# Moving the first four gate tiles of an RG-LRU branch forward among a projection's matmuls, with new pools

## The chip, the cores and the metric

The kernel runs on one core of one Trainium2 chip. Its time is the device time in microseconds (us) from one execution; of several executions the median is given. The engines that matter are TensorE (PE, the matmuls), VectorE (DVE), ScalarE (ACT) and GpSimd (POOL); SyncE (SP) issues most of the DMAs, ACT a few.

## The reference: one layer of a hybrid recurrent decoder

576 tokens (one prompt of 512 and 8 samples of 8) of width 1024 go through one layer. One projection of the normed input yields the columns of three branches and of three merge gates; each branch ends in a SiLU gate and an output projection, and the merged sum goes through one more.

```python
u, za, xb, zb, q, zc, gates = split_in(xn @ w_in)
oa = rwkv7_branch(u, za, ...); ob = rglru_branch(xb, zb, ...); oc = cross_attn(q, zc, mem_k, mem_v)
merged = g_a * (oa @ w_br_a) + g_b * (ob @ w_br_b) + g_c * (oc @ w_br_c)
y = x + merged @ w_out
```

The branch that the change touches is the RG-LRU ("Hawk"): a causal convolution of width 4 over `xb`, two block-diagonal gates, a linear recurrence over time, and the product with SiLU(zb):

```python
xc = conv_b + sum(ext[:, j:j + t] * cw[j] for j in range(4))
a = exp(-8 * sigmoid(xc @ w_rg_a + b) * softplus(-lam))
b = sqrt(1 - a * a) * sigmoid(xc @ w_rg_x + b2) * xc
h_t = a_t * h_(t-1) + b_t;  out = h * silu(z)
```

## The kernel before: a stream of projections with everything else between

**The stream.** Every big projection is cut into units of 128 output columns. A unit (class `Unit`, run by `Stream.step`, L355) has 8 steps, one for each 128 rows of the contraction; a step is 6 matmuls of 288 tokens (three products of high and low parts, two halves of the tokens), so a unit is 48 matmuls. Its weights are loaded by SP (`wraw`), rounded by ACT (`whi`, L280), and the rest is made by DVE (`wlo`, L281); the stream does this for the next unit when a unit starts, if a next unit is queued. A unit writes one of two PSUM buffers and ends in a `use`: for `zb` a tanh on ACT and a multiply on DVE (L410, L411) and a store to DRAM; for a branch unit `br` one multiply on DVE (L448 or L450), and for the middle branch an addition on POOL (L452). `st.go(n)` emits n steps, `st.until(label)` emits until a unit is done.

**The order of work** at the end of the kernel: the RWKV phase, among whose operations the units of the gates, of `zc` and `xb` and the first two of `zb` run; the other six `zb` units; 8 units `br2` (branch c, "first", which write `merged`), 8 units `br0` (branch a, "mid"), 8 units `br1` (branch b, the LRU's, "last"), and the output projection (L1345). `br1` needs the LRU's output `ob` as high and low parts (`oh`, `ol`).

**The LRU phase** (`lru_phase`, L468 on) works on 8 tiles of 128 channels. For tile j, `conv(j)` loads `xe` (issued by ACT, L490), and makes `xc` with one ACT and four DVE instructions (L496 to L502) and two small POOL copies; `gates(j)` is 4 small products on PE (`pg`, L516; the trace shows 8 records), 4 tanh on ACT (L517), three DVE instructions (L521, L530, L532) and four more ACT ones (L525 to L529), and leaves the decay `ae`, the gated input `gx` and the argument of a root; `roots` takes the square roots of four tiles in one ACT instruction (L557); `scan(j)` makes `be` on POOL (L542 to L544), runs the recurrence on DVE (L546), copies two state columns on POOL (L548, L549), multiplies with the gate path `z` on DVE (L551, L552) and splits the product into `oh` and `ol` (L592 on ACT, L593 on DVE). `load_split` loads a branch's output from DRAM and splits it in the same way.

**What sets the order.** The program text gives each instruction its rank; a planner then simulates the engines with its own costs and writes each engine's queue: an instruction that it takes to be ready can pass one of a higher rank that is not. The queues are fixed in that order before the kernel runs, and each engine keeps its order. Tiles live in pools; a tile whose buffer or memory is still in use waits for the last reader of the one before.

In the kernel before, `lru_phase` is called when all `zb` units are written and the input `xh`, `xl` is released (`xstack.close()`). Its main loop is

```python
for j in range(4):
    conv(j); st.go(9 if j else 13); gates(j)
    if j == 3: then()
    st.go(3)
st.until("br27"); roots(0)
for j in range(4, KC):
    conv(j); st.go(4); scan(j - 4); st.go(3); gates(j); st.go(3)
roots(4)
for j in range(4, KC):
    scan(j); st.go(9)
```

Of the kernel before, what the change touches and what calls it, by code (L numbers as in the profile page):

```python
# [9 lines left out]
F32 = mybir.dt.float32  # L10
F32R = mybir.dt.float32r
I32 = mybir.dt.int32
AF = mybir.ActivationFunctionType
ALU = mybir.AluOpType
# [4 lines left out]
P = 128  # L19
D = 1024  # L20
KC = 8
TP = 512
NB = 8
NS = 8
N = TP + NB * NS
# [359 lines left out]
def smp(t):  # L385
    return t[:, TP:N].rearrange("p (b s) -> p b s", s=NS)
# [78 lines left out]
        split(nc, oh[:, k, :], ol[:, k, :], t)  # L465


def lru_phase(K, o2, then):  # L468
    nc, tc, i, pv = K.nc, K.tc, K.i, K.pv
    st = K.st  # L470
    lo_st = K.cst.tile([P, 9, 8], F32, name="lru_st")
    cv_st = K.cst.tile([P, 9, 3, 8], F32, name="conv_st")
    with tc.tile_pool(name="lruc", bufs=1, reuse_waits="tile") as lc, tc.tile_pool(name="lru", bufs=2, reuse_waits="tile") as lp:
        wbd = []
        for q, nm in enumerate(("w_rg_a", "w_rg_x")):
            w = lc.tile([P, KC, P], F32, name=f"wbd{q}")
            nc.gpsimd.memset(w, 0.0)
            src = i[nm][0].rearrange("(j two) i o -> two i j o", two=2)
            for h in range(2):
                nc.scalar.dma_start(w[64 * h:64 * h + 64, :, 64 * h:64 * h + 64], src[h])  # L480
            wbd.append(w)
        AE = TP + NB * 9
        ohl = []
        sl = K.par[:, K.off["state_lru"]:K.off["state_lru"] + 64].rearrange("p (b j) -> p b j", j=8)
        xcs, keep, args, quad = {}, {}, {}, {}

        def conv(j):
            xe = lp.tile([P, XE], F32, tag="xe", name="xe")
            xp, xs = token_ext(xe, 3)
            nc.scalar.dma_start(xe, K.xbd[j])  # L490
            nc.gpsimd.tensor_copy(cv_st[:, 0, :, j], xp[:, TP:TP + 3])
            nc.gpsimd.tensor_copy(cv_st[:, 1:9, :, j], xs[:, :, NS:NS + 3])
            t = lp.tile([P, XE], F32, tag="cva", name="cva")
            M = XE - 3
            cw = [pv("conv_w", r * 8 + j) for r in range(4)]
            nc.scalar.activation(t[:, :M], xe[:, 0:M], AF.Identity, scale=cw[0], bias=pv("conv_b", j))  # L496
            for r in (1, 2):
                nc.vector.scalar_tensor_tensor(t[:, :M], xe[:, r:r + M], cw[r], t[:, :M], op0=ALU.mult, op1=ALU.add)
            xc = lp.tile([P, N], F32, tag="xc", name="xc")
            nc.vector.scalar_tensor_tensor(xc[:, 0:TP], xe[:, 3:3 + TP], cw[3], t[:, 0:TP], op0=ALU.mult, op1=ALU.add)  # L500
            ts = t[:, 515:515 + 88].rearrange("p (b s) -> p b s", s=11)[:, :, 0:8]
            nc.vector.scalar_tensor_tensor(smp(xc), xs[:, :, 3:], cw[3], ts, op0=ALU.mult, op1=ALU.add)  # L502
            xcs[j] = xc

        def gates(j):
            if j % 4 == 0:
                quad[j // 4] = lp.tile([P, 4, N], F32, tag="args", name="args")
            ar = args[j] = quad[j // 4][:, j % 4, :]
            xc = xcs[j]
            gs = []  # L510
            for q, bh in enumerate((K.bah, K.bxh)):
                g = lp.tile([P, N], F32, tag=f"g{q}", name=f"g{q}")
                for s in range(2):
                    pg = K.psb(f"pg{q}")[:, 0:HN]
                    cs = slice(HN * s, HN * s + HN)
                    nc.tensor.matmul(pg, wbd[q][:, j, :], xc[:, cs], start=True, stop=True)  # L516
                    nc.scalar.activation(g[:, cs], pg, AF.Tanh, bias=bh[:, j:j + 1], scale=0.5)  # L517
                gs.append(g)
            gr, gi = gs
            c4 = K.c4[:, j:j + 1]  # L520
            nc.vector.tensor_scalar(gr, gr, c4, c4, op0=ALU.mult, op1=ALU.add)  # L521
            ae = lp.tile([P, AE], F32, tag="ae", name="ae", bufs=4)
            ap_, as_ = token_ext(ae, 0, 9)
            nc.gpsimd.memset(as_[:, :, 0:1], 0.0)
            nc.scalar.activation(ap_, gr[:, 0:TP], AF.Exp)  # L525
            nc.scalar.activation(as_[:, :, 1:9], smp(gr), AF.Exp)
            th = lp.tile([P, AE], F32, tag="th", name="th")[:, 0:N]
            nc.scalar.activation(th, gr, AF.Tanh, scale=-1.0)
            nc.scalar.activation(gr, gr, AF.Exp, scale=2.0)  # L529
            nc.vector.scalar_tensor_tensor(ar, gr, 1.0, th, op0=ALU.add, op1=ALU.mult)  # L530
            gx = lp.tile([P, N], F32, tag="gx", name="gx", bufs=4)
            nc.vector.scalar_tensor_tensor(gx, gi, 1.0, xc, op0=ALU.add, op1=ALU.mult)  # L532
            keep[j] = (ae, gx)

        def scan(j):
            ar = args[j]
            ae, gx = keep[j]
            z2 = o2.tile([P, N], F32, tag="gtt", name="z2", bufs=5)
            K.dma(z2, K.zbd[j])
            be = lp.tile([P, AE], F32, tag="th", name="be")  # L540
            bp_, bs_ = token_ext(be, 0, 9)
            nc.gpsimd.tensor_copy(bs_[:, :, 0:1], sl[:, :, j:j + 1])  # L542
            nc.gpsimd.tensor_mul(bp_, ar[:, 0:TP], gx[:, 0:TP])
            nc.gpsimd.tensor_mul(bs_[:, :, 1:9], smp(ar), smp(gx))  # L544
            he = lp.tile([P, XE], F32, tag="cva", name="he")[:, 0:AE]
            nc.vector.tensor_tensor_scan(he, ae, be, 0.0, op0=ALU.mult, op1=ALU.add)  # L546
            hp_, hs_ = token_ext(he, 0, 9)
            nc.gpsimd.tensor_copy(lo_st[:, 0, j:j + 1], hp_[:, TP - 1:TP])  # L548
            nc.gpsimd.tensor_copy(lo_st[:, 1:9, j:j + 1], hs_[:, :, 8:9])  # L549
            o = lp.tile([P, N], F32, tag="g0", name="lo")  # L550
            nc.vector.scalar_tensor_tensor(o[:, 0:TP], hp_, 0.5, z2[:, 0:TP], op0=ALU.mult, op1=ALU.mult)  # L551
            nc.vector.scalar_tensor_tensor(smp(o), hs_[:, :, 1:9], 0.5, smp(z2), op0=ALU.mult, op1=ALU.mult)  # L552
            split(nc, ohl[0][:, j, :], ohl[1][:, j, :], o)

        def roots(j0):
            q4 = quad[j0 // 4]
            nc.scalar.activation(q4, q4, AF.Sqrt, scale=0.25)  # L557

        for j in range(4):
            conv(j)  # L560
            st.go(9 if j else 13)
            gates(j)
            if j == 3:
                then()
            st.go(3)
        st.until("br27")
        ohl = [o2.tile([P, KC, N], F32R, tag=tag, name=tag) for tag in ("oh", "ol")]
        roots(0)
        for j in range(4, KC):
            conv(j)  # L570
            st.go(4)
            scan(j - 4)
            st.go(3)
            gates(j)
            st.go(3)
        roots(4)
        for j in range(4, KC):
            scan(j)
            st.go(9)
    lf = lo_st.rearrange("p a b -> p (a b)")  # L580
    K.rows_out(lf, [(0, 72, [(0, 8, K.o["lru_p"].rearrange("a b (j c) -> (a b j) c", c=P)),
                             (8, 64, K.o["lru_s"].rearrange("a b (j c) -> (a b j) c", c=P))])])
    cf = cv_st.rearrange("p a r b -> p (a r b)")
    cs = K.o["conv_s"].rearrange("a b r (j c) -> (a b r j) c", c=P)
    K.rows_out(cf, [(0, 120, [(0, 24, K.o["conv_p"].rearrange("a b r (j c) -> (a b r j) c", c=P)), (24, 96, cs[0:96])]),
                    (120, 96, [(0, 96, cs[96:192])])])
    return ohl
# [795 lines left out]
def hybrid_step(ctx: ExitStack, tc: tile.TileContext, ins, outs):  # L1383
    nc = tc.nc
    K = Kern(ctx, tc, ins, outs)
    st = K.st = Stream(K)

    def pool(stack, name, bufs=1, **kw):
        return stack.enter_context(tc.tile_pool(name=name, bufs=bufs, reuse_waits="tile", **kw))
# [52 lines left out]
    rwkv_phase(K)  # L1442
    for j in range(KC):
        st.until(f"zc{j}")
    K.merged = pool(ctx, "mg").tile([P, KC, N], F32, name="merged")
    o2 = pool(ctx, "o2", bufs=2)

    def operand():
        return [o2.tile([P, KC, N], F32R, tag=tag, name=tag) for tag in ("oh", "ol")]

    oc, oa = operand(), operand()
    load_split(K, o2, K.ocz, *oc)
    for j in range(KC):
        st.until(f"zb{j}")
    xstack.close()
    st.add(*branch_units(K, o2, 2, ins["w_br_c"][0], *oc, "first"))
    st.add(*branch_units(K, o2, 0, ins["w_br_a"][0], *oa, "mid"))
    ob = lru_phase(K, o2, lambda: load_split(K, o2, K.oad, *oa))
    st.until("br07")
    mhl = operand()  # L1460
    st.add(*branch_units(K, o2, 1, ins["w_br_b"][0], *ob, "last", mhl))
    with ExitStack() as es:
        fp = pool(es, "fin")
# [40 lines left out]
```

## Time and profile before

| | |
|---|---|
| time, median of 3 | 1185.82 us (1184.57 to 1187.84) |
| the profiled execution's own time | 1189.67 us |
| its span, first to last instruction | 1187.9 us |
| PE busy | 1151.5 us (97%) |
| DVE, ACT, POOL busy | 711.5, 516.0, 182.7 us |
| mean granted TensorE clock | 0.992 |

In the profile a row of the timeline gives start, duration, engine, line, operation, output and inputs, how many instructions are merged in the row, and in brackets the idle time before it with the instruction that ended it. Matmuls overlap, so the rhythm of PE is read from one start to the next. A group row gives busy time, the mean duration in ns, and the idle time before the group with what ended it. In a table by stretches the columns are the length and then, for PE, weight loads, DVE, ACT and POOL, the busy time with the number of instructions; then the granted clock, the DMA share and GB/s.

### The profile page before, as it was taken

The page shows a single profiled execution, that of the slowest core. Times are in us where ns is not written, and L with a number is a line of the kernel's source. Part 1 is how long each engine was busy: PE and PEld are TensorE (multiplying, and loading weights), DVE is VectorE, ACT ScalarE, POOL GpSimd, SP SyncE. Part 2 cuts the span into 40 slices and gives each one's busy share as a digit, 9 for nine tenths or more (in the row PEclk, how much of TensorE's full clock was granted, in tenths as well). Part 3 has the DMA queues.
Part 4 walks back from the last instruction along what each step waited for, and adds up shares of the span by engine and source line. Part 5 has one row for each costly group of instructions (what it writes and reads, how often), then busy time and mean ns, then how long its engine had stood idle before and what let it go on. Part 6 is the DMA issues. An engine that isn't in the chain of part 4 may idle for free.

```text
span 1187.9 us, 25753 instructions
## 1 busy us (share of the span) xinstructions
PE 1151.5 (97%) x10599; PEld 1070.9 (90%) x10599; DVE 711.5 (60%) x1435; ACT 516.0 (43%) x1003; POOL 182.7 (15%) x311
## 2 busy tenths in 40 slices
PE   6999999999999999999999999999999999989997
PEld 4998877898998898988989988999889999979997
DVE  5445655238754687735788457875355386875633
ACT  5444544337224473243742335622434366542333
POOL 3010001010003210022100130102211011570032
PEclk9999999999999999999999999999999999999999
DMA  4447685532342222432224522254336666338412
GB/s 139 129 142 226 219 252 189 158 89 79 87 134 78 68 88 77 139 87 65 72 84 134 136 81 66 82 145 128 98 99 206 202 209 180 104 105 268 112 50 81
DMA packets 219344, 150.99 MB, mean 127 GB/s; under 512 B 52384, under 2 KB 194826, under 8 KB 219226
## 3 DMA queue, kind: packets, MB, share of 16 engines
q1 hardware_dynamic: 215962, 146.34, 42.1%
q10 hardware_dynamic: 3264, 2.99, 0.9%
q8 instruction: 84, 1.38, 0.5%
q14 instruction: 34, 0.28, 0.1%
HBM read 120.29 MB, written 29.01 MB: 126 GB/s over the span
## 4 chain that ended last, share of the span: by engine, by line
PE 81%; DVE 7%; ACT 4%; issue 3%; DMA 3%; POOL 1%; SPq 0%; DVEq 0%; ACTq 0%
PE u L355 13%; PE g L355 12%; PE br L355 9%; PE za L355 5%; PE xb L355 4%; PE zc L355 4%; PE q L355 4%; PE fo L1345 4%; PE zb L355 3%; PE kv L355 2%; PE dS L1133 1%; PE m L986 1%; DVE wlo L281 1%; DMA wraw<-in_w_mem_kv 1%; PE skt L64 1%
## 5 line engine op out<-in xcount | busy, mean ns | idle before, releaser
L280 ACT CAST whi<-wraw 128x1024 fp32r<-128x1024 f32 x129 | 135.4, 1050 | 300.6 <-PE g L355 87.9
L281 DVE TENSOR_TENSOR wlo<-wraw,whi 128x1024 fp32r<-128x1024 f32 x128 | 158.4, 1237 | 130.7 <-ACT whi L280 123.6
L355 PE MATMUL u<-xh,whi 128*128 128x288 f32 x400 | 93.3, 307 | 0.0
L355 PE MATMUL u<-xh,wlo 128*128 128x288 f32 x400 | 89.6, 299 | 0.0
L355 PE MATMUL u<-xl,whi 128*128 128x288 f32 x400 | 88.5, 299 | 0.0
L355 PE MATMUL br<-oh,whi 128*128 128x288 f32 x384 | 85.0, 303 | 3.0 <-ACT oh L592 2.9
L355 PE MATMUL br<-oh,wlo 128*128 128x288 f32 x384 | 83.8, 300 | 4.0 <-DVE wlo L281 4.0
L355 PE MATMUL g<-xh,whi 128*128 128x288 f32 x384 | 85.8, 302 | 0.0
L355 PE MATMUL g<-xh,wlo 128*128 128x288 f32 x384 | 84.4, 298 | 0.0
L355 PE MATMUL g<-xl,whi 128*128 128x288 f32 x384 | 84.4, 299 | 0.0
L355 PE MATMUL br<-ol,whi 128*128 128x288 f32 x384 | 83.7, 300 | 0.0
L355 PEld LDWEIGHTS u<-xh,whi 128*128 128x128 f32 x400 | 65.0, 188 | 6.9 <-issue 5.3
L355 PEld LDWEIGHTS br<-oh,wlo 128*128 128x128 f32 x384 | 62.7, 192 | 5.4 <-DVE wlo L281 5.3
L355 PEld LDWEIGHTS br<-oh,whi 128*128 128x128 f32 x384 | 63.2, 192 | 4.3 <-ACT oh L592 3.4
L355 PEld LDWEIGHTS u<-xh,wlo 128*128 128x128 f32 x400 | 65.2, 188 | 0.8
L355 PEld LDWEIGHTS u<-xl,whi 128*128 128x128 f32 x400 | 64.9, 188 | 0.8 <-issue 0.4
L355 PEld LDWEIGHTS g<-xh,whi 128*128 128x128 f32 x384 | 61.7, 188 | 3.3 <-issue 3.1
L355 PEld LDWEIGHTS g<-xl,whi 128*128 128x128 f32 x384 | 62.1, 188 | 1.6 <-issue 1.6
L355 PEld LDWEIGHTS br<-ol,whi 128*128 128x128 f32 x384 | 63.1, 192 | 0.1
L355 PEld LDWEIGHTS g<-xh,wlo 128*128 128x128 f32 x384 | 62.2, 188 | 0.9 <-issue 0.9
L1012 DVE TENSOR_TENSOR Xt<-X 72x30 f32<-72x30 f32 (+14 forms) x120 | 39.4, 328 | 13.6 <-DMA X<-d 9.9
L1345 PE MATMUL fo<-wol,oh 128*128 128x256 f32 (+1 forms) x160 | 45.0, 282 | 0.0
(388 smaller groups left out, 2895.3 us busy)
## 6 DMA issues: line engine op xcount, KB each, us to landing
wraw<-in_w_in SPq DMA_DIRECT2D x89, 512.0 KB
wraw<-in_w_mem_kv SPq DMA_DIRECT2D x16, 512.0 KB
kn<-in_cache_mem_k SPq DMA_DIRECT2D x16, 512.0 KB
kn<-in_cache_mem_v SPq DMA_DIRECT2D x16, 512.0 KB
gd<-flt SPq DMA_DIRECT2D x24, 288.0 KB
gtt<-gd SPq DMA_DIRECT2D x24, 288.0 KB
wraw<-in_w_br_c SPq DMA_DIRECT2D x8, 512.0 KB
wraw<-in_w_br_a SPq DMA_DIRECT2D x8, 512.0 KB
```

The lines of the kernel that those rows point to most:

```text
L64: self.nc.tensor.transpose(out, in_, self.ident[:rows, :rows])
L280: nc.scalar.copy(hi, raw)
L281: eng.tensor_sub(lo, raw, hi.bitcast(F32))
L355: nc.tensor.matmul(self.ps[:, o:o + m], a[:, k, :], b[:, k, t0:t0 + m], start=(k == 0 and q == 0), stop=(k == KC - 1 and q == 2))
L986: nc.tensor.matmul(pms[h][64 * w:64 * w + 64, P * (c - c0):P * (c - c0) + P], BK[64 * h:64 * h + 64, c, w, :], ZR[64 * h:64 * h + 64, c].r ...
L1012: nc.vector.tensor_mul(tv, X[:, 0:s, s:s + 1].to_broadcast([NQ, s, m]), X[:, s:s + 1, s + 1:].to_broadcast([NQ, s, m]))
L1133: nc.tensor.matmul(pS[hs, C * o.q:C * o.q + C], o.BKn[:, c, hs], o.UV[:, c, hs], start=True, stop=True, tile_position=(0, 64 * h))
L1345: nc.tensor.matmul(pos[t][:r, :W], a[:, k, t * P:t * P + r], b[:, k, :], start=(k == 0 and q == 0), stop=(k == KC - 1 and q == 2))
```

## The change

`lru_phase` is now called before the six remaining `zb` units have been emitted. The convolutions and gates of tiles 0 to 3 are emitted among these units (6 steps, gates, 4 steps for each tile: 40 of 48 steps). Then `zb` is finished, `merge()` releases `xh` and `xl`, allots `merged` and the operand of branch a in the place of the input, and queues `br2` and `br0`. The scans of tiles 0 to 3 follow with 3 steps between, the convolutions and gates of tiles 4 to 7 with 5, `load_split` of branch a (`then()`), and the scans of tiles 4 to 7 with 4. A scan no longer splits its result: the product is written over `gx`, which has 8 buffers now, and after `br27` the 8 splits are emitted together, with 3 steps between, among the `br0` units. The root's argument has one buffer of four tiles where it had two; `oh`, `ol` of branch c are in a pool of one buffer, which the LRU's operand takes over, and those of branch a are in another, which the merged operand takes over.

```diff
-def lru_phase(K, o2, then):
+def lru_phase(K, o2, merge, operand):
...
-                quad[j // 4] = lp.tile([P, 4, N], F32, tag="args", name="args")
+                quad[j // 4] = lp.tile([P, 4, N], F32, tag="args", name="args", bufs=1)
...
-            gx = lp.tile([P, N], F32, tag="gx", name="gx", bufs=4)
+            gx = lp.tile([P, N], F32, tag="gx", name="gx", bufs=8)
...
-            o = lp.tile([P, N], F32, tag="g0", name="lo")
-            nc.vector.scalar_tensor_tensor(o[:, 0:TP], hp_, 0.5, z2[:, 0:TP], op0=ALU.mult, op1=ALU.mult)
-            nc.vector.scalar_tensor_tensor(smp(o), hs_[:, :, 1:9], 0.5, smp(z2), op0=ALU.mult, op1=ALU.mult)
-            split(nc, ohl[0][:, j, :], ohl[1][:, j, :], o)
+            nc.vector.scalar_tensor_tensor(gx[:, 0:TP], hp_, 0.5, z2[:, 0:TP], op0=ALU.mult, op1=ALU.mult)
+            nc.vector.scalar_tensor_tensor(smp(gx), hs_[:, :, 1:9], 0.5, smp(z2), op0=ALU.mult, op1=ALU.mult)
...
         for j in range(4):
             conv(j)
-            st.go(9 if j else 13)
+            st.go(6)
             gates(j)
-            if j == 3:
-                then()
+            st.go(4)
+        for j in range(KC):
+            st.until(f"zb{j}")
+        oa, then = merge()
+        st.go(2)
+        roots(0)
+        for j in range(4):
+            scan(j)
             st.go(3)
-        st.until("br27")
-        ohl = [o2.tile([P, KC, N], F32R, tag=tag, name=tag) for tag in ("oh", "ol")]
-        roots(0)
+            if j == 2:
+                conv(4)
         for j in range(4, KC):
-            conv(j)
-            st.go(4)
-            scan(j - 4)
-            st.go(3)
             gates(j)
-            st.go(3)
+            if j < 7:
+                conv(j + 1)
+            st.go(5)
+        then()
         roots(4)
         for j in range(4, KC):
+            st.go(4)
             scan(j)
-            st.go(9)
+        st.until("br27")
+        ohl = operand(o2)
+        for j in range(KC):
+            split(nc, ohl[0][:, j, :], ohl[1][:, j, :], keep[j][1])
+            st.go(3)
...
-    K.merged = pool(ctx, "mg").tile([P, KC, N], F32, name="merged")
-    o2 = pool(ctx, "o2", bufs=2)
...
+    o2 = pool(ctx, "o2")
...
     load_split(K, o2, K.ocz, *oc)
-    for j in range(KC):
-        st.until(f"zb{j}")
-    xstack.close()
-    st.add(*branch_units(K, o2, 2, ins["w_br_c"][0], *oc, "first"))
-    st.add(*branch_units(K, o2, 0, ins["w_br_a"][0], *oa, "mid"))
-    ob = lru_phase(K, o2, lambda: load_split(K, o2, K.oad, *oa))
+    o3 = []
+
+    def merge():
+
+        xstack.close()
+        K.merged = pool(ctx, "mg", side="right").tile([P, KC, N], F32, name="merged")
+        o3.append(pool(ctx, "o3", side="right"))
+        oa = operand(o3[0])
+        st.add(*branch_units(K, o2, 2, ins["w_br_c"][0], *oc, "first"))
+        st.add(*branch_units(K, o2, 0, ins["w_br_a"][0], *oa, "mid"))
+        return oa, lambda: load_split(K, o2, K.oad, *oa)
+
+    ob = lru_phase(K, o2, merge, operand)
     st.until("br07")
-    mhl = operand()
+    mhl = operand(o3[0])
     st.add(*branch_units(K, o2, 1, ins["w_br_b"][0], *ob, "last", mhl))
```

More of the change, by code (lines that the diff above doesn't have):

```diff
@@ L482, in lru_phase @@
         AE = TP + NB * 9
-        ohl = []
         sl = K.par[:, K.off["state_lru"]:K.off["state_lru"] + 64].rearrange("p (b j) -> p b j", j=8)
@@ L1444, in hybrid_step, with operand @@
         st.until(f"zc{j}")
-    K.merged = pool(ctx, "mg").tile([P, KC, N], F32, name="merged")
-    o2 = pool(ctx, "o2", bufs=2)
-    def operand():
-        return [o2.tile([P, KC, N], F32R, tag=tag, name=tag) for tag in ("oh", "ol")]
-    oc, oa = operand(), operand()
-    load_split(K, o2, K.ocz, *oc)
-    for j in range(KC):
-        st.until(f"zb{j}")
-    xstack.close()
-    st.add(*branch_units(K, o2, 2, ins["w_br_c"][0], *oc, "first"))
-    st.add(*branch_units(K, o2, 0, ins["w_br_a"][0], *oa, "mid"))
-    ob = lru_phase(K, o2, lambda: load_split(K, o2, K.oad, *oa))
+    o2 = pool(ctx, "o2")
+    def operand(pl):
+        return [pl.tile([P, KC, N], F32R, tag=tag, name=tag) for tag in ("oh", "ol")]
+    oc = operand(o2)
+    load_split(K, o2, K.ocz, *oc)
+    o3 = []
[8 more added lines that the diff above has]
+    ob = lru_phase(K, o2, merge, operand)
     st.until("br07")
-    mhl = operand()
+    mhl = operand(o3[0])
     st.add(*branch_units(K, o2, 1, ins["w_br_b"][0], *ob, "last", mhl))
```

## The prediction, made before the change was run

> **What bounds the kernel now.** I read the page's busy shares first, then the busy times by stage at the end of the kernel, then what PE waited for there, and last the timelines of PE and DVE around those waits.
>
> ```profile
> span 1187.9 us, 25753 instructions
> PE 1151.5 (97%) x10599; PEld 1070.9 (90%) x10599; DVE 711.5 (60%) x1435; ACT 516.0 (43%) x1003; POOL 182.7 (15%) x311
> ```
>
> PE is the bound: 36.4 us of the span is all that it idles, and no reordering can win more than that plus what a lower clock costs. The change touches only what follows the RWKV phase. By stage (the last `zb` units, `br2`, `br0` up to its sixth unit, the end of the LRU, `br1` up to the output projection):
>
> ```profile
> 903.50:942.10 38.60, 38.60 (x292) 38.60 (x291) 17.82 (x21) 15.14 (x23) 0.00 (x0) 1.00 0.75 242
> 942.10:1001.50 59.40, 59.40 (x422) 57.71 (x421) 44.75 (x61) 37.04 (x58) 8.39 (x24) 1.00 0.61 184
> 1001.50:1049.20 47.70, 47.00 (x322) 44.40 (x320) 39.76 (x48) 26.80 (x47) 23.47 (x27) 1.00 0.45 128
> 1049.20:1071.80 22.60, 15.59 (x100) 14.41 (x100) 17.46 (x20) 7.07 (x8) 18.15 (x21) 0.92 0.36 105
> 1071.80:1128.00 56.20, 56.20 (x414) 56.20 (x415) 31.48 (x37) 16.07 (x21) 2.33 (x1) 0.97 0.64 190
> ```
>
> PE is without a gap in the `zb` and `br2` stages, and loses 7.0 of 22.6 us in the fourth. There, and in the first microseconds of the fifth, the granted clock (the third number from the end) is below 1. What PE waited for from 880 us to 1130 us:
>
> ```profile
> PE br L355 <- DVE wlo L281: 4.0, 4, 3.0
> PE br L355 <- ACT oh L592: 2.9, 1, 2.9
> PE ro L64 <- POOL lru_st L549: 0.7, 1, 0.7
> ```
>
> and PE's own timeline in that place:
>
> ```profile
> 1048.50 0.43 PE L355 MATMUL br<-ol,whi 128*128 128x288 f32 x2
> ...
> 1058.32 0.63 PE L355 MATMUL br<-oh,whi 128*128 128x288 f32 x2 [2.92 <-ACT oh L592]
> ...
> 1059.80 0.85 PE L355 MATMUL br<-oh,wlo 128*128 128x288 f32 x2 [0.37 <-DVE wlo L281]
> ...
> 1061.88 0.46 PE L355 MATMUL br<-oh,whi 128*128 128x288 f32 x2
> ...
> 1066.43 0.43 PE L355 MATMUL br<-oh,wlo 128*128 128x288 f32 x2
> 1067.55 0.30 PE L64 MATMUL ro<-ident,lru_st 128*72 128x128 f32 x1 [0.69 <-POOL lru_st L549]
> ...
> 1071.72 0.53 PE L355 MATMUL br<-oh,wlo 128*128 128x288 f32 x2 [2.96 <-DVE wlo L281]
> ...
> 1075.74 0.43 PE L355 MATMUL br<-oh,wlo 128*128 128x288 f32 x2
> ```
>
> The idle time is 2.92 + 0.37 + 0.69 + 2.96 = 6.94 us. After each long gap matmuls come at about half the rate. The ordinary rhythm is 34 matmuls in the 4.55 us from 1061.88 to 1066.43, 0.134 us each (a unit of 48: 6.4 us). The 12 started between 1058.32 and 1061.88 took 3.56 - 0.37 = 3.19 us where 1.61 was due; the 18 between 1071.72 and 1075.74 took 4.02 where 2.41 was due. That is 1.58 + 1.61 = 3.19 us more, so the place costs 10.1 us in all.
>
> Why PE stands still is seen in DVE's queue:
>
> ```profile
> 1048.02 1.21 DVE L281 TENSOR_TENSOR wlo<-wraw,whi 128x1024 fp32r<-128x1024 f32 x1
> 1052.82 2.44 DVE L546 TENSOR_TENSOR_SCAN he<-ae,be 128x584 f32<-128x584 f32 x1 [3.59 <-POOL be L544]
> 1055.41 1.37 DVE L546 TENSOR_TENSOR_SCAN he<-ae,be 128x584 f32<-128x584 f32 x1 [0.15 <-POOL be L544]
> ...
> 1057.43 0.74 DVE L450 SCALAR_TENSOR_TENSOR gtt<-gtt,br 128x576 f32<-128x576 f32 x1
> 1058.09 1.65 DVE L281 TENSOR_TENSOR wlo<-wraw,whi 128x1024 fp32r<-128x1024 f32 x1
> ...
> 1070.45 1.21 DVE L281 TENSOR_TENSOR wlo<-wraw,whi 128x1024 fp32r<-128x1024 f32 x1
> ```
>
> The scan of tile 4 stands at the head of DVE's queue and waits 3.59 us for POOL. Behind it are the L450 that frees a unit's PSUM buffer, and the next unit's `wlo`. PE restarts at 1058.32, just after that L450, although the row names ACT's `oh`; and at 1071.72 just after the `wlo`. So the stall is the order of DVE's queue while the scans are crammed in front of `br1`, not a lack of DVE time over the whole end. The second scan stands ahead of the L450 though the text has it behind: the planner reorders by its own clock, and the written step counts are only ranks.
>
> **The change, part by part.** The profiled execution took 1189.67 us (span 1187.9, 1.8 around it), 3.9 above the median of 1185.82; I take differences from its rows and put them on the median.
>
> *Scans of tiles 4 to 7 no longer end at `br1`.* They are ranked inside `br2`, their splits among `br0`, and 40 of `br0`'s 64 steps follow the last split. So nothing of the LRU is left when `br1` comes, and the first `wlo` of `br1` has a quiet DVE. All four waits and both slow stretches go: -10.1 us. The waits of 0.3 us that follow pass with them or stay; I count them as nothing.
>
> *Convolutions and gates of tiles 0 to 3 move into the `zb` stage.* What DVE does for them, over all eight tiles, with the scans:
>
> ```profile
> L498 DVE SCALAR_TENSOR_TENSOR cva<-xe,par,cva 128x600 f32<-128x600 f32 x16 | 14.5, 910 | 1.7 <-ACT cva L496 1.6
> L546 DVE TENSOR_TENSOR_SCAN he<-ae,be 128x584 f32<-128x584 f32 x8 | 13.2, 1655 | 9.4 <-POOL be L544 9.4
> L532 DVE SCALAR_TENSOR_TENSOR gx<-g,xc 128x576 f32<-128x576 f32 x8 | 7.2, 895 | 0.7 <-ACT g L517 0.6
> L500 DVE SCALAR_TENSOR_TENSOR xc<-xe,par,cva 128x512 f32<-128x512 f32 x8 | 7.1, 890 | 0.4
> L530 DVE SCALAR_TENSOR_TENSOR args<-g,th 128x576 f32<-128x576 f32 x8 | 6.6, 825 | 2.2 <-ACT g L529 2.2
> ...
> L521 DVE TENSOR_SCALAR g<-g,c 128x576 f32<-128x576 f32 x8 | 5.7, 715 | 3.6 <-ACT g L517 3.5
> L551 DVE SCALAR_TENSOR_TENSOR lo<-he,z 128x512 f32<-128x512 f32 x8 | 5.4, 681 | 0.0
> ...
> L552 DVE SCALAR_TENSOR_TENSOR lo<-he,z 128x64 f32<-128x64 f32 x8 | 2.9, 366 | 0.0
> L502 DVE SCALAR_TENSOR_TENSOR xc<-xe,par,cva 128x64 f32<-128x64 f32 x8 | 2.3, 286 | 0.0
> ```
>
> Convolutions and gates: 14.5 + 7.2 + 7.1 + 6.6 + 5.7 + 2.3 = 43.4 us, 21.7 for four tiles. PE's part is the same four `pg` groups in another place:
>
> ```profile
> 956.18 1.94 PE pg L516 x8
> ```
>
> so the `zb` stage becomes 38.6 + 4 x 1.94 = 46.4 us long and DVE has 17.8 + 21.7 = 39.5 us in it. It fits, and costs PE nothing while it does. If it starts late, some of it runs on into `br2`; that cover is the next part's. It can start late: the block weights `wbd` come over ACT's queue, behind the splits of branch c, which wait for their loads:
>
> ```profile
> 911.88 2.90 ACT L592 CAST oh<-oxl 128x576 fp32r<-128x576 f32 x4 [0.33 <-DMA oxl<-ocz]
> ...
> 921.57 0.60 ACTq L480 DMA_DIRECT2D wbd<-in_w_rg_x  x1
> ```
>
> The four moved `xe` loads are issued on the same queue, behind these. So the first gates are likelier in the fourth `zb` unit than at step 6 of the first, and the last ones end near the end of `zb`. PE does not mind: the planner puts a `pg` where it takes it to be ready. SP's queue gets the four `z` loads of the first scans earlier, behind the `zb` stores; they are needed only after a scan.
>
> *Scans 0 to 7 and convolutions and gates 4 to 7 in `br2`.* This is the price. `br2` had 44.75 us of DVE work in 59.4 us. It loses 21.7 and gains as much, and gets eight scans on top: 13.2 + 5.4 + 2.9 = 21.5 us. That makes 66.3 us in 59.4, with durations that include how POOL and DVE stretch one another (the scan took 2.44 us beside POOL, 1.37 else). The wait of scans for POOL, 9.4 us in the group row, comes to it where the planner has nothing to put there. One new wait is added: with one buffer for the root's arguments, L530 of tile 4 waits until POOL has read those of tiles 0 to 3; behind it on DVE are again an L448 and a `wlo`, for which PE waits. PE bears a lag of about 5.5 us (in the rows above, L450 came 8.5 us after its unit's last matmul, which ended at 1048.9 and PE lost 2.9). So the cost lies between 0 (DVE's spare 6.9 us in `zb`, and scans that slide into `br0`, where the splits leave room) and 66.3 + 9.4 - 59.4 = 16.3 us, if nothing slides and no lag is left. The nearest row is the stall of the same chain before, roots then POOL then scan with `br` work behind: 2.92 + 0.37 + 1.58 = 4.9 us. Two such chains stand in `br2` now; the one for tiles 0 to 3 cost nothing before, with its scans spread out. I take one stall: +4.9.
>
> *The rest* is without a price: eight splits move into `br0`, whose DVE gives up scans, convolutions and gates; no instruction is added; the operand's buffers are handed on at the same ends of `br2` and `br0` as before; the root's table changes stay three, as long as `roots` is not put between two tanh of `zb`.
>
> Sum: -10.1 + 4.9 = -5.2 us, 1180.6 us.
>
> **A rule against the change.** POOL's product for the next scan ran beside that scan of 2.44 us; and what else POOL did in the old `br0`:
>
> ```profile
> 1052.75 1.28 POOL L543 TENSOR_TENSOR be<-args,gx 128x512 f32<-128x512 f32 x1
> ```
>
> ```profile
> L452 POOL TENSOR_TENSOR merged<-merged,gtt 128x576 f32<-128x576 f32 x7 | 13.5, 1931 | 9.0 <-DVE gtt L450 9.0
> ```
>
> The Trainium skill ("SBUF — State Buffer", section "Who interferes with whom") says that a DVE instruction with two SBUF inputs and a GpSimd instruction that reads SBUF exclude one another, the later one fully blocked. That scan agrees. By it every scan's POOL work in `br2` would hold up a convolution or a `wlo`, which is the fourth rival's side. Against that, `br2` has none of those additions, 13.5 us of POOL's time beside the old scans.
>
> **The rivals.**
> 1. *No new stall* (0.30). The planner hoists scans 0 to 3 into `zb` and lets 4 to 7 slide. For it: 39.5 of 46.4 us in `zb`, and `br0` without a gap up to its sixth unit at 39.76 of 47.7. Against: 66.3 in 59.4. 1185.8 - 10.1 = 1175.7.
> 2. *The forecast, one stall* (0.31): 1180.6, its own range 1178.5 to 1183.
> 3. *The stall is only moved* (0.21): both root chains stall PE, 2 x 4.9 - 10.1 = -0.3, 1185.5. This is also what comes out if the gates start so late that they do not leave `br2`, so that the change does not do what it says.
> 4. *DVE becomes the bound of `br2`* (0.18): each unit waits for its L448 and `wlo`, and the stage ends when DVE does, 16.3 us late. It decides against the change from 10.1 us on. -10.1 + 16.3 = +6.2, 1192.0. For it: the sum of 66.3 and the waits; against: `br0` and `br1` leave DVE half idle, and the ranks of late scans are low.
>
> **How the numbers follow.** What this kernel's times can tell from no change is about 0.3%, 3.6 us. Faster: rival 1, and the forecast but for its worse end, 0.30 + 0.26 = 0.56. Slower: rival 4, and a little of 3, 0.19. The rest, 0.25, is within. The range from 1174 to 1190 leaves out the best end of rival 1 and the worse half of rival 4.
>
> **What would show it.** Right: no PE gap over 0.5 us between 1040 us and the output projection; `pg` groups among the `zb` matmuls; the `oh` casts of the LRU well before `br1`'s first matmul; a gap or two in `br2`, each ahead of a DVE L448 or `wlo` behind a scan. Wrong: `br2` without any gap (rival 1), gaps at every unit of `br2` with DVE above 95% (rival 4), or gaps of PE ahead of `pg` in `zb`, for which I have no term.

## The result: 0.6% slower, and the profile after

The changed kernel takes 1196.6 us (median of 7, 1190.08 to 1197.79) against 1185.82: a ratio of 1.0059 on record, 95% interval 1.0039 to 1.0079. The quotient of the two medians is larger, 1.0091; the text goes by the ratio, which agrees with the profiled pair (7.1 us more) and with a second run of the same text, 1.0067, 1.0042 to 1.0091 (e13 below). The forecast was 1180.6, and the time lies above the whole range of 1174 to 1190. Ratios leave out the few executions at a much lower clock, such as two of e17's nine (1811 and 1558 us at a granted clock of 0.56 and 0.65).

The page of the profiled execution after (1197.31 us, span 1195.0):

```profile
span 1195.0 us, 25763 instructions
PE 1151.4 (96%) x10599; PEld 1069.8 (90%) x10599; DVE 707.6 (59%) x1435; ACT 514.7 (43%) x1003; POOL 183.4 (15%) x311
```

Over the whole span PE is busy as long as before, 1151.4 us against 1151.5, and idle for 43.6 us where it was 36.4. What PE waited for in the changed part, 880 to 1140 us (us in total, times, longest):

```profile
PE pg L517 <- DVE xc L501: 6.2, 2, 3.7
PE br L355 <- DVE wlo L281: 3.5, 3, 1.7
PE br L355 <- DVE merged L448: 2.1, 1, 2.1
PE pg L517 <- POOL conv_st L493: 1.7, 1, 1.7
...
PE br L355 <- DVE flt L411: 0.4, 1, 0.4
```

These sum to 13.9 us; the same view of before had 7.6. PE's timeline shows where they stand: two in the `zb` stage, three around the scans of tiles 0 to 3, three around those of tiles 4 to 7.

```profile
922.59 2.18 PE L517 MATMUL pg<-xc,wbd 128*128 128x288 f32 x8 [1.71 <-POOL conv_st L493]
...
932.44 1.24 PE L517 MATMUL pg<-xc,wbd 128*128 128x288 f32 x2 [2.49 <-DVE xc L501]
...
962.66 0.50 PE L355 MATMUL br<-oh,whi 128*128 128x288 f32 x2 [0.39 <-DVE flt L411]
...
965.09 0.54 PE L355 MATMUL br<-oh,wlo 128*128 128x288 f32 x2 [1.68 <-DVE wlo L281]
...
974.92 4.21 PE L517 MATMUL pg<-xc,wbd 128*128 128x288 f32 x8 [3.69 <-DVE xc L501]
...
1013.35 0.54 PE L355 MATMUL br<-oh,wlo 128*128 128x288 f32 x2 [1.55 <-DVE wlo L281]
...
1021.58 0.50 PE L355 MATMUL br<-oh,whi 128*128 128x288 f32 x2 [2.11 <-DVE merged L448]
1022.62 0.53 PE L355 MATMUL br<-oh,wlo 128*128 128x288 f32 x2 [0.29 <-DVE wlo L281]
```

So `zb` lost 1.71 + 2.49 = 4.2 us, the first chain of scans 0.39 + 1.68 + 3.69 = 5.8, the second 1.55 + 2.11 + 0.29 = 3.9. By stage (the `zb` units; most of `br2`; two stretches up to the output projection; the columns as in the stages of before):

```profile
902.90:955.70 52.80, 48.59 (x323) 45.94 (x321) 35.44 (x49) 35.02 (x60) 4.58 (x14) 0.97 0.62 199
955.70:1022.60 66.90, 57.22 (x374) 53.31 (x372) 55.35 (x72) 36.34 (x57) 29.57 (x44) 0.95 0.51 153
1022.60:1080.00 57.40, 57.38 (x431) 57.36 (x432) 25.85 (x29) 13.47 (x19) 17.65 (x9) 1.00 0.65 198
1080.00:1131.30 51.30, 51.30 (x387) 51.30 (x386) 27.16 (x31) 15.08 (x17) 2.44 (x1) 1.00 0.44 124
```

After 1022.6 us PE has no gap and a full clock: the old stall at the border of `br0` and `br1` is gone, as forecast. In the second stage PE loses 9.7 us although DVE is busy in only 55.35 of 66.9. DVE's queue shows why:

```profile
957.89 3.98 DVE L547 TENSOR_TENSOR_SCAN he<-ae,be 128x584 f32<-128x584 f32 x2 [3.83 <-POOL be L545]
961.79 0.73 DVE L411 SCALAR_TENSOR_TENSOR flt<-flt,zb 128x576 f32<-128x576 f32 x1
...
963.70 1.33 DVE L281 TENSOR_TENSOR wlo<-wraw,whi 128x1024 fp32r<-128x1024 f32 x1
...
965.83 2.47 DVE L547 TENSOR_TENSOR_SCAN he<-ae,be 128x584 f32<-128x584 f32 x1
...
970.75 0.83 DVE L499 SCALAR_TENSOR_TENSOR cva<-xe,par,cva 128x600 f32<-128x600 f32 x1
...
974.12 0.74 DVE L501 SCALAR_TENSOR_TENSOR xc<-xe,par,cva 128x512 f32<-128x512 f32 x1
...
1009.66 2.44 DVE L547 TENSOR_TENSOR_SCAN he<-ae,be 128x584 f32<-128x584 f32 x1 [1.02 <-POOL be L545]
1012.02 1.27 DVE L281 TENSOR_TENSOR wlo<-wraw,whi 128x1024 fp32r<-128x1024 f32 x1
...
1016.71 1.38 DVE L547 TENSOR_TENSOR_SCAN he<-ae,be 128x584 f32<-128x584 f32 x1 [1.40 <-POOL be L545]
...
1020.69 0.74 DVE L448 SCALAR_TENSOR_TENSOR merged<-gtt,br 128x576 f32<-128x576 f32 x1
```

A scan stands at the head of the queue and waits for POOL, and behind it stand the L411 and L448 that free PSUM buffers and the `wlo` of the next unit. PE goes on just after the `wlo` at 963.70, after the one at 1012.02 and after the L448 at 1020.69. What the first scan waited for is on ACT and POOL:

```profile
952.79 1.28 ACT L556 ACT_TABLE_LOAD   x1
954.09 2.13 ACT L556 ACTIVATE args<-args 128x2304 f32<-128x2304 f32 x1
956.23 1.28 ACT L410 ACT_TABLE_LOAD   x1
957.53 0.65 ACT L410 ACTIVATE flt<-zb 128x576 f32<-128x576 f32 x1
...
966.00 0.89 ACT L497 ACTIVATE cva<-xe,par 128x600 f32<-128x600 f32 x1 [6.88 <-POOL lru_st L550]
```

```profile
956.29 1.29 POOL L544 TENSOR_TENSOR be<-args,gx 128x512 f32<-128x512 f32 x1 [3.31 <-ACT args L556]
```

One root over four tiles, then POOL's product of 1.29 us, then the scan. Of the scan's wait of 3.83 us, 2.2 pass before the root is done at 956.22; the rest is POOL. The last ACT row is a second consequence: the convolution of tile 4 waits 6.88 us, because its buffer `cva` is shared with a scan's result `he`, which POOL's copy L550 had still to read. That convolution's `xc` (974.12) is what PE's longest gap, 3.69 us, ended with.

### The profile page after: what moved, and what is told of

It reads as the page before. It is cut to its first block, busy times and chain, and to the rows that moved or that the text cites. A ratio compares the mean times of both kernels' runs of the same rounds, so it can differ in the third digit from the quotient of the medians.

```text
span 1195.0 us, 25763 instructions
## 1 busy us (share of the span) xinstructions
PE 1151.4 (96%) x10599; PEld 1069.8 (90%) x10599; DVE 707.6 (59%) x1435; ACT 514.7 (43%) x1003; POOL 183.4 (15%) x311
## 4 chain that ended last, share of the span: by engine, by line
PE 79%; DVE 7%; ACT 6%; DMA 4%; issue 3%; POOL 1%; SPq 0%; DVEq 0%; ACTq 0%
PE u L355 13%; PE g L355 12%; PE br L355 10%; PE za L355 4%; PE xb L355 4%; PE zc L355 4%; PE q L355 4%; PE fo L1353 4%; PE kv L355 2%; PE dS L1141 1%; PE m L994 1%; DVE wlo L281 1%; PE skt L64 1%; DMA wraw<-in_w_mem_kv 1%; ACT whi L280 1%
```

## The experiments

Ratios are to the kernel before, run beside each, with 95% intervals. Each edit is made in the changed kernel unless it says otherwise. "Gaps" are waits of PE in the changed part.

**The changed kernel again (e13).** No edit.

> The changed kernel itself, beside the other runs of this group. Theory: 1.004 to 1.008, with the waits ahead of pg in zb and the gaps of both scan chains as in its first profile. Rival (its first time was of that chip or that hour): below 1.003.

Measured 1.0067 (1.0042 to 1.0091), 14.0 us of gaps in the same places. What the profile after shows comes back in a second run.

**e1: the early gates undone, the rest of the change kept.**

```
+        for j in range(KC):
+            st.until(f"zb{j}")
+        oa, then = merge()
+        then()
...
-        for j in range(KC):
-            st.until(f"zb{j}")
-        oa, then = merge()
...
```

> The changed kernel with one part undone: the convolutions and gates of tiles 0 to 3 are emitted after the zb units again, among br2; the new pools, the four scans in a row and the late splits stay, and tiles 4 to 7 come among br0. Theory (the loss is three places of the changed kernel, each with its own cause: two waits of PE for xc in zb, 4.2 us and about 1.4 us of half clock; the chain roots-scan of tiles 0 to 3, 5.8 and 2.5; that of tiles 4 to 7, 3.9): the zb stage is free of gaps, the two chains stall as before, 5.6 us better than the changed kernel, ratio to the kernel before about 1.001 to 1.004. Rival (DVE has too much work in br2, and the early gates relieve it): the zb gaps go, but br2 and br0 stall more, no better than the changed kernel, 1.006 or above.

Measured 1.0064 (1.0049 to 1.0079). Its longest waits from 880 to 1140 us:

```profile
PE br L355 <- DVE wlo L281: 11.1, 2, 6.1
PE zb L355 <- DVE flt L411: 1.7, 1, 1.7
PE zb L355 <- DVE wlo L281: 1.0, 1, 1.0
```

The rival's time came: without the early gates the kernel is as slow as with them, and `zb` is not free of gaps. The rival's cause, too much DVE work in `br2`, is not shown by this; e7 and e11 speak against it. The two chains stall PE for 5.0 and 6.1 us, and again a scan waits for POOL's product in front of a `wlo`:

```profile
987.23 2.44 DVE L547 TENSOR_TENSOR_SCAN he<-ae,be 128x584 f32<-128x584 f32 x1 [3.31 <-POOL be L545]
...
993.77 1.24 DVE L281 TENSOR_TENSOR wlo<-wraw,whi 128x1024 fp32r<-128x1024 f32 x1
```

Gates in `zb` are thus neither the whole loss nor a gain that can be seen. The pair does not isolate them, though: in e1 the second chain (scans from 1035.14 to 1047.64) stands among the L450 of `br0`, not in `br2`.

**e2 and e3: the scans spread out.** e2 gives the roots' arguments four tiles of their own and emits scan j-4, convolution j and gates j in turn. e3 emits scans 4 to 7 behind `br2` again, four steps apart, between the splits of tiles 0 to 3.

```
-            if j % 4 == 0:
-                quad[j // 4] = lp.tile([P, 4, N], F32, tag="args", name="args", bufs=1)
-            ar = args[j] = quad[j // 4][:, j % 4, :]
+            ar = args[j] = lp.tile([P, N], F32, tag="args", name="args", bufs=4)
...
```

> The changed kernel with the scans of tiles 0 to 3 spread among the convolutions and gates of tiles 4 to 7 (scan, 3 steps, convolution, 2 steps, gates, 3 steps), the same 34 steps in all. For this the root's arguments are four tiles of one column tile each instead of one of four, with four small root instructions for each half. Theory (the chain of tiles 0 to 3 stalls PE because four scans stand in a row ahead of the convolution of tile 4): the gap ahead of pg of tile 4 (3.7 us) and those of 0.4 and 1.7 us before it go, 8 us better than the changed kernel, ratio to the kernel before 0.998 to 1.001. Rival (DVE is simply overfull in br2): the gaps move to other units of br2, the sum of them stays at 5 us or more, 1.005 or above.

```
+        st.until("br27")
+        ohl = operand(o2)
         roots(4)
         for j in range(4, KC):
-            st.go(4)
             scan(j)
+            st.go(4)
+            split(nc, ohl[0][:, j - 4, :], ohl[1][:, j - 4, :], keep[j - 4][1])
+            st.go(4)
...
```

> The changed kernel with roots and scans of tiles 4 to 7 after br27, among br0, each followed by the split of an earlier tile. Theory: the waits of 1.55, 2.1 and 0.3 us at the end of br2 go, nothing else changes, 4 us better than the changed kernel, ratio to the kernel before 1.002 to 1.004. Rival (POOL's additions in br0 stretch the scans as they did in the kernel before): the stall comes back in br0 or ahead of br1 with 3 us or more, 1.006.

e2: 1.0044 (1.0026 to 1.0062). The 9.7 us of gaps in `br2` became 8.1, in other places, mostly ahead of `pg`: the stall is moved, not dissolved. e3: 1.0037 (1.0020 to 1.0054), within the theory's range, but the edit did not do what it says. The planner still ran the four scans from 1006.71 to 1019.71 us, ahead of the last two L448 of `br2`; in the changed kernel they ran from 1009.66 to 1023.85. The second chain's 3.9 us fell to one gap of 1.7; the first chain's longest stayed at 3.7. So no run with the early gates has scans in `br0`.

**e4, e14: the waits in `zb`.** e4 emits the load and split of branch c after the gates of tile 1; e14 gives the conv inputs `xe` three buffers for two, and the tag `gtt` four for five to make room.

```
+            if j == 1:
+                load_c()
...
-    load_split(K, o2, K.ocz, *oc)
...
```

> The changed kernel with the loads and splits of branch c emitted after the gates of tile 1 instead of before the convolution of tile 0. Theory (the first convolution stands behind eight casts on ACT that wait for their loads: the load of xe landed at 911.1 us, its ACT instruction ran at 916.2): the wait of 1.7 us ahead of the first pg goes or shrinks below 0.5 us; the waits for xe of tile 2 (2.5 us) and the later stalls stay; 2 us better than the changed kernel, ratio 1.004. Rival (it is the loads themselves that are slow there): the first pg waits as long as before, 1.006.

```
-            xe = lp.tile([P, XE], F32, tag="xe", name="xe")
+            xe = lp.tile([P, XE], F32, tag="xe", name="xe", bufs=3)
...
```

> The changed kernel with three buffers for xe instead of two, and four for the tiles gtt, oxl and z instead of five, for room. Theory (the waits for xc in zb are late loads of xe: 5.5 and 6.0 us for tiles 1 and 2, where the kernel before had 2.9 to 4.4; tile 2 is loaded only when tile 0 is read): the load of tile 2 is issued earlier, the wait of 2.5 us goes, 2 to 4 us better than the changed kernel. Rival (ACT's and DVE's queues make xc late, whenever the load lands): the wait stays above 1.5 us.

e4: 1.0006 (0.9988 to 1.0025); e14: 1.0005 (0.9992 to 1.0018). In both the second gap of `zb`, 2.49 us, is gone (0.27 in e4), and the first stays at 1.35 and 1.19. In the changed kernel ACT shows what was late ahead of the second, the load of tile 2:

```profile
922.79 0.33 ACTq L491 DMA_DIRECT2D xe<-xbd  x1
...
928.80 0.89 ACT L497 ACTIVATE cva<-xe,par 128x600 f32<-128x600 f32 x1 [3.49 <-DMA xe<-xbd]
```

With a third buffer that load is issued at 917.33 us and waits for nothing. In e4 it is not earlier (924.73), and why the planner's order there has no such gap was not followed. e4 gained more than the theory gave it; its gaps sum to 9.7 us.

**e5: the scan's result out of the convolutions' buffer.**

```
-            he = lp.tile([P, XE], F32, tag="cva", name="he")[:, 0:AE]
+            he = lp.tile([P, AE], F32, tag="g0", name="he")
```

> The changed kernel with the scan's result he in the buffers of the tag g0 instead of those that it shares with the convolution's sum (cva, two buffers). Theory (the convolution of tile 4 could not start on ACT until a scan's result was read: its ACT instruction waited 6.9 us, and the first pg of tile 4 cost PE 3.7 us): the wait ahead of that pg falls below 1 us, the other gaps stay, 4 us better than the changed kernel, ratio to the kernel before 1.002 to 1.004. Rival (the row of scans on DVE delays this convolution anyway): the wait stays above 2.5 us, 1.005 to 1.007.

Measured 1.0026 (1.0013 to 1.0039). The 3.69 us wait ahead of tile 4's `pg` is below 0.5, so the shared buffer was its cause. Another wait grew in the second chain:

```profile
PE br L355 <- DVE merged L448: 3.6, 1, 3.6
```

**e6: e4 and e3 together.**

> The two changes that helped put together: the splits of branch c after the gates of tile 1, and the scans of tiles 4 to 7 in br0. Theory (the places add): the waits at the end of br2 shrink to one of under 2 us, the zb stage keeps about 1.5 us, the chain of tiles 0 to 3 its 5 to 6; 2 us better than the splits alone, ratio to the kernel before 0.997 to 1.000. Rival (they were run-to-run differences, or the stall comes back elsewhere): 1.001 or above.

Measured 1.0007 (0.9992 to 1.0022): no better than e4 alone, though the second chain's gaps are nearly gone (its scans, too, are still in `br2`). Gaps of 2.88, 2.14 and 3.98 us stand earlier in its place.

**e7: the product `be` from POOL to DVE.** This adds 16 instructions to the engine that rival 4 held to be full.

```
-            nc.gpsimd.tensor_mul(bp_, ar[:, 0:TP], gx[:, 0:TP])
-            nc.gpsimd.tensor_mul(bs_[:, :, 1:9], smp(ar), smp(gx))
+            nc.vector.tensor_mul(bp_, ar[:, 0:TP], gx[:, 0:TP])
+            nc.vector.tensor_mul(bs_[:, :, 1:9], smp(ar), smp(gx))
```

> The changed kernel with the two products that make be moved from POOL to DVE, 16 instructions; DVE has about 0.7 + 0.2 us more for each scan (by the rows of args), 7 us in all. Theory (the scans hold up br's wlo and L448 because they wait for POOL at the head of DVE's queue and are stretched beside POOL's work, 2.44 us against 1.37): the chains stall PE less, the gaps in br2 fall from 9.7 us to 5 or less, ratio to the kernel before 0.999 to 1.003. Rival (DVE has too much work in br2, whatever it waits for): the gaps grow by some of the 7 us, 1.007 or above.

Measured 0.9990 (0.9976 to 1.0005), 0.7% off the changed kernel's ratio: the largest gain of a single edit, though the intervals of e4 and e14 overlap with it. The groups of the scans and of the products behind them on DVE, first in the changed kernel, then here, where `be` is a DVE group too (busy us, mean ns, idle time before them):

```profile
L547 DVE TENSOR_TENSOR_SCAN he<-ae,be 128x584 f32<-128x584 f32 x8 | 14.2, 1776 | 6.4 <-POOL be L545 6.2
L551 DVE SCALAR_TENSOR_TENSOR gx<-he,z 128x512 f32<-128x512 f32 x8 | 7.2, 900 | 0.0
```

```profile
L547 DVE TENSOR_TENSOR_SCAN he<-ae,be 128x584 f32<-128x584 f32 x8 | 11.0, 1370 | 0.0
L551 DVE SCALAR_TENSOR_TENSOR gx<-he,z 128x512 f32<-128x512 f32 x8 | 5.5, 687 | 0.0
L544 DVE TENSOR_TENSOR be<-args,gx 128x512 f32<-128x512 f32 x8 | 5.5, 684 | 3.8 <-ACT args L556 3.8
```

and e7's page:

```profile
PE 1146.6 (97%) x10599; PEld 1066.2 (90%) x10599; DVE 706.6 (60%) x1451; ACT 515.2 (43%) x1003; POOL 165.7 (14%) x295
```

The scans no longer wait for POOL, and a scan is 1370 ns long, not 1776. The head of DVE's queue still waits, 3.8 us where it was 6.2: now `be` waits there for ACT's root. DVE does 16 instructions more in 1.0 us less busy time. The edit thus shortens the wait by 2.4 us, scans and L551 by 3.2 + 1.7 us, and lets the planner order the queue anew; no run tells these apart.

**e8 and e10: the same edit in the kernel before**, e10 with the LRU's state rows written out after `br12` besides.

```
+        st.until("br12")
+        lru_rows()
...
```

> The kernel before with the same two products on DVE. Theory (as for the changed kernel): the scans of tiles 4 to 7 no longer wait for POOL behind its additions, the stall of 6.9 us and its 3.2 us of half clock shrink to half, ratio 0.994 to 0.998. Rival (too much DVE work ahead of br1): the stall grows, 1.000 to 1.005.

> The kernel before with be on DVE and the state rows of the LRU put out after the third br1 unit instead of ahead of br1. With be on DVE alone PE waited 6.7 us ahead of br1 for POOL's copies of the state columns. Theory (that wait is the last of the stall): the gaps of PE fall from 8.4 us to 2 us, and the half clock behind them goes, 7 to 9 us better than the kernel before, ratio 0.992 to 0.995. Rival (br1 would then wait for the LRU's output in the same place): the gap is ahead of br1's first or later steps instead, 0.997 to 0.999.

e8: 0.9986 (0.9973 to 0.9999). The theory's ratio was missed, since the stall took another form:

```profile
PE ro L64 <- POOL lru_st L549: 6.7, 1, 6.7
```

PE's transposes of the state rows wait for POOL's small copies, and these for the last scan, which ran on DVE at 1061.36 us behind two splits, a `wlo` and its own `be`. e10 takes these transposes later: 0.9950 (0.9935 to 0.9966), with gaps of 1.69 and 3.33 us left where its theory had 2 us.

**e9, e11, e15, e16: the edits together.** e11 has `be` on DVE, `he` in `g0` and branch c's split later; e9 has also e3's edit; e15 and e16 leave one of e11's edits out.

> All that helped the changed kernel, together: be on DVE, the splits of branch c after the gates of tile 1, the scan's result in g0, the scans of tiles 4 to 7 in br0. Theory (the causes are separate): PE's gaps from zb to the output projection fall to 4 us or less in all, ratio to the kernel before 0.994 to 0.998. Rival (they are the same slack counted several times): no better than be on DVE alone, 0.998 to 1.001.

> As the kernel with all that helped, but the scans of tiles 4 to 7 in br2 as in the changed kernel. Theory (with be on DVE a scan waits for nothing, and a place in br2 costs as little as one in br0): within 0.2% of it. Rival (DVE is too full in br2): 2 us or more slower than it, gaps ahead of L448 or wlo at the end of br2.

> The changed kernel with be on DVE and the scan's result in g0. Theory (the parts add: be on DVE 0.999, the splits of branch c about 0.005, he in g0 the rest): 0.995 to 0.998, the wait ahead of pg of tile 4 gone, those in zb as in the changed kernel. Rival (he is worth nothing once scans do not wait): 0.999.

> The changed kernel with be on DVE and the splits of branch c after the gates of tile 1. Theory: 0.993 to 0.996, the second wait in zb gone, the one ahead of pg of tile 4 still about 2 us. Rival (the splits are worth nothing once scans do not wait): 0.999.

e11: 0.9910 (0.9895 to 0.9926), 1178.77 us, the fastest of all kernels here. e9: 0.9943 (0.9925 to 0.9961), 0.3% slower, more than the 0.2% that e11's theory allowed; its scans of tiles 4 to 7, from 997.31 to 1007.57 us, were still in `br2`, so it does not test `br0` either. e15: 0.9963 (0.9950 to 0.9976), e16: 0.9948 (0.9930 to 0.9966): leaving out the later split or the move of `he` costs 0.4 to 0.5%. e11's profiled span is 1176.8 us. In the same stretches of time in which the changed kernel lost 4.2 and 9.7 us of PE (not quite the same work, since e11 is ahead), e11 has:

```profile
902.90:955.70 52.80, 51.06 (x356) 48.99 (x355) 42.56 (x63) 40.09 (x66) 7.10 (x19) 1.00 0.70 216
955.70:1022.60 66.90, 66.87 (x476) 64.89 (x475) 60.28 (x92) 36.48 (x60) 12.55 (x27) 1.00 0.62 185
```

In the second DVE is fuller than in the changed kernel (60.28 us against 55.35), and PE is as good as never idle. So it was not DVE's amount of work that held PE. A wait at the head is left even here, twice for ACT's root (2.21 and 1.65 us), and PE bears it.

**e12: e1 with `be` on DVE.**

> The kernel with the first four tiles' gates after the zb units, and be on DVE. It tells whether the early gates are worth anything once the scans no longer wait for POOL. Theory (the stalls of 5.0 and 6.1 us in that kernel were scans that waited for POOL and were stretched by it): they fall below 2 us each, ratio 0.997 to 1.000, no slower than the changed kernel with be on DVE (0.999). Rival (without the early gates DVE is too full in br2 and br0): the gaps stay above 3 us each, 1.003 or above.

Measured 1.0002 (0.9986 to 1.0018), against 0.9990 (0.9976 to 1.0005) for e7, which has the early gates. The stalls of 5.0 and 6.1 us fell to 2.14 and 3.29, not below 2 as the theory had it. By this pair the early gates' own worth is not to be told from nothing; but here, as in e1, the second chain is in `br0`.

**e17, e18: the first gates eight steps later**, in e11 and in the changed kernel, for the one gap that e11 still has (1.74 us ahead of the first `pg`).

```
-            st.go(6)
+            st.go(6 if j else 14)
```

> The version with the product on DVE, he in g0 and branch c's split later (1178.8 us, ratio 0.9910) has one gap of PE left, 1.74 us ahead of the first pg; in its trace the xc of tile 0 (L501) stood on DVE 3.3 us behind a convolution step of tile 1 that waited for tile 1's load. Here the first gates are emitted 14 stream steps after the first convolution and not 6, eight steps or about 6.4 us later. Theory (the first pg stands in PE's order earlier than xc can be there): the gap is below 0.5 us, ratio 0.989 to 0.991. Rival (the planner puts the pg where it takes xc to be ready, whatever the step count says, and takes the load to land too early): a gap of 1 to 2.5 us stays, ratio 0.990 to 0.993.

> The changed kernel with the first gates emitted 14 steps after the first convolution and not 6. Theory (the first pg stands too early): the first gap of 1.71 us is below 0.5, the others stay at some 12 us, ratio to the kernel before 1.004. Rival (the planner reorders by its own clock): a first gap of 1 to 2.5 us stays, ratio 1.005 to 1.007. A shift of all later work by 6 us could also lengthen the stall of the first scan chain, 5.8 us: then above 1.008.

The rival's gaps came: 1.58 and 1.42 us stay. Eight steps are 6.4 us, but the first `pg` comes at 917.11 us in e17 (918.76 in e11) and at 919.91 in e18 (922.59 in the changed kernel). The count of steps is only a rank: the `pg` came no later for it. e17's ACT and DVE show what it waited for:

```profile
908.06 0.33 ACTq L491 DMA_DIRECT2D xe<-xbd  x1
...
914.58 0.89 ACT L497 ACTIVATE cva<-xe,par 128x600 f32<-128x600 f32 x1 [2.23 <-DMA xe<-xbd]
```

```profile
915.50 0.84 DVE L499 SCALAR_TENSOR_TENSOR cva<-xe,par,cva 128x600 f32<-128x600 f32 x1 [2.28 <-ACT cva L497]
916.26 0.75 DVE L501 SCALAR_TENSOR_TENSOR xc<-xe,par,cva 128x512 f32<-128x512 f32 x1
```

The `xe` of tile 1 takes 6.5 us from issue to use; tile 1's L499 waits for it at the head of DVE's queue, and tile 0's `xc` (L501), for which PE waits until 917.11, stands behind it. That is in e17 and e11; in the changed kernel and e18 there are splits of branch c and `zb` work before that L501 instead. Ratios: e18 1.0054 (1.0035 to 1.0073), as the rival had it. e17 0.9950 (0.9931 to 0.9970), above both forecasts and worse than e11's 0.9910 though its profiled span is only 1.1 us longer, 1177.9; the traces do not explain that. The two ran on different chips, so e11's gain is safest given as 0.5 to 0.9%.

## Why the prediction was wrong, step by step

*The old stall goes, -10.1 us: right.* No gap of PE and a clock of 1.00 from 1022.6 us up to the output projection at 1131.3.

*"It fits, and costs PE nothing while it does": failed.* The `zb` stage cost 4.2 us of gaps, and 3.4 us at half clock behind the second of them. The working compared 39.5 us of DVE work with 46.4 us of PE time, and left the rest to the sentence "PE does not mind: the planner puts a `pg` where it takes it to be ready". PE did mind: the `pg` stood in its queue before `xc` was there. In front of the first one `xc` was late behind branch c's splits, in front of the second behind the load of tile 2, which waited for a buffer (e14). A planner that takes these to be ready too soon would do that; its own times are not on record. In PE's trace no `zb` matmul passes the waiting `pg`. That the first gates would come in the fourth unit was right (922.59 us), and that the loads would be late was in the prediction, with their queue; that PE would wait was listed only as a sign of being wrong.

*"I take one stall: +4.9": mis-sized.* Both chains stalled, 5.8 and 3.9 us, 9.7 in all, and the clock was halved for 6.8 us behind the longest gap. Rival 3, at a chance of 0.21, had the two stalls, at 9.8 with 3.2 us of slow clock in it; it had nothing for `zb`. The argument for one was that the chain of tiles 0 to 3 "cost nothing before, with its scans spread out". The change puts those four scans together, since one buffer for the roots' arguments forces all of them ahead of the gates of tile 4. Spreading them (e2) only took 9.7 us of gaps to 8.1. Part of the 5.8, the gap of 3.69, came by a way that the prediction had not: not L530's wait for the arguments, but `he` and `cva` in one buffer (e5).

*The sum.* From the first matmul of the `zb` stage to the first of the output projection the kernel before took 220.45 us (903.54 to 1123.99), the changed one 228.41 (902.90 to 1131.31): +8.0 us where the forecast had -5.2. PE's idle time in it rose from 7.7 to 13.9 us, its busy time for the same matmuls from 212.8 to 214.5. The longer busy time goes with the clock: it is 0.50 from 932.5 to 935.9 us and from 973.5 to 980.3, behind the gaps of 2.49 and 3.69, and 1.00 in the rest, where the kernel before had two short slow stretches. Outside this part the changed kernel was 0.9 us quicker, which makes the 7.1 of the spans. (The prediction's last stage, drawn to 1128.0 us, runs 4 us into the output projection; nothing in its sum rests on that.)

*Rival 4, DVE as the bound of `br2`: its time of 1192.0 was the nearest, by luck, its mechanism wrong.* DVE never was the bound. With 16 more instructions on it the kernel is faster (e7), and at 60.28 of 66.9 us it holds up nothing (e11). The sum "66.3 in 59.4" counted durations some of which are shorter without POOL (a scan 1655 ns there, 1370 in e7); that alone does not make it fit, and where the rest went was not followed.

*"The table changes stay three, as long as `roots` is not put between two tanh of `zb`": it was put there.* Rows 952.79 to 957.53 show it, with 1.28 us for a load. The changes still are three, at 952.79, 956.23 and 1004.55 us: the return to tanh moved from a gate into `zb`. It cost PE little that shows: the L411 behind that tanh started at 961.79, when the scans ahead of it on DVE were done, 3.6 us after the tanh.

*The rule against the change.* In the changed kernel a scan took 1776 ns in the mean, and 1370 when POOL had no product beside it (e7). The Trainium skill ("SBUF — State Buffer", section "Who interferes with whom") lets a DVE instruction with two SBUF inputs and a GpSimd instruction that reads SBUF exclude one another. The traces agree, with 0.4 us a scan. With L551 (900 ns and 687) that is 3.2 + 1.7 = 4.9 us of DVE time, more than the 2.4 us by which the wait at the head fell. The prediction weighed against this rule that `br2` has none of POOL's additions; the products alone stretched scans and L551 this far.

**What stays open.** Whether early gates are worth anything. e7 against e12 shows no gain, with the second chain in another place; e11 (0.9910) against the best version of the old order, e10 (0.9950), says some 0.4%, but e10 lacks e11's other edits, and e17 at 0.9950 takes the gain back. Which part of e7's edit helped, the shorter wait, the shorter scans or the new order, is open, and so is what scans in `br0` would do beside early gates. The time that the planner assumes for an `xe` load was not changed in any run, so that its correction would close the last gap is only argued.

## What to carry to other kernels

A sum of work against a stage's length does not show what an in-order queue holds up: before moving a chain that crosses engines (root on ACT, product on POOL, scan on DVE) into a busy stage, look at what is queued behind each of its waits and how long its links are beside the other engine, and try short links on one engine. A step count in an emitted order is no time where a planner reorders (e3, e17), so look in the trace where the moved work ran before reading its time. And when tiles share a buffer tag, list whose last read comes before whose first write, across the moved parts too.

## What the runs showed of the hardware that was not expected

*A product is shorter on DVE than on POOL, and cost DVE's total nothing.* It took 1.29 us on POOL in the row above and 684 ns on DVE in e7. With the products on it DVE's busy time over the kernel was 706.6 us against 707.6, since scans and L551 became 4.9 us shorter.

*Some gaps of 2 us slow PE's clock, and some do not.* Four stretches of 20 us of the changed kernel, the granted clock third from the end:

```profile
920.00:940.00 20.00, 15.79 (x84) 13.64 (x83) 14.62 (x22) 13.88 (x28) 1.18 (x4) 0.91 0.53 181
960.00:980.00 20.00, 14.24 (x79) 12.43 (x78) 18.57 (x25) 5.87 (x9) 10.82 (x19) 0.84 0.54 171
1000.00:1020.00 20.00, 17.92 (x133) 17.44 (x131) 15.96 (x19) 10.71 (x14) 12.95 (x16) 1.00 0.62 194
1020.00:1040.00 20.00, 18.13 (x134) 17.93 (x135) 15.62 (x21) 6.97 (x11) 4.81 (x6) 1.00 0.58 166
```

The first two hold the gaps of 2.49 and 3.69 us (with smaller ones) and lost clock; the last two hold those of 1.55 and 2.11 and lost none, nor did e11 with its 1.74. In the trace before, gaps of 2.92 and 2.96 us lost it too. The other traces give no sharp limit. Over the 4 us behind each gap from 880 to 1140 us, every one of 2.33 us or more lowered the clock, none of 0.9 to 1.95 us did that stood alone, and between these both occur: e7's 1.99 us left 0.68, e16's 2.27 left 1.00. The Trainium skill ("TensorE: Matmul & The Clock Gate", Part 1) puts the loss after an idle window of about 3.4 us that runs freely; the gap of 2.49 us is shorter than that, and the measurement decides here.
